# One PSUM tile of eight banks for a whole transformer-block kernel, in place of three pools

## The chip, the cores and the metric

The kernel runs on one core of one Trainium2 chip. The metric is device time in microseconds of one execution. Five engines matter: PE (TensorE) multiplies matrices and writes its sums to PSUM; DVE (VectorE), ACT (ScalarE) and POOL (GpSimd) compute on elements; SP (SyncE) issues most of the DMA transfers. PSUM has eight banks of 512 float32 per partition; one matmul of this kernel fills at most one bank.

## The reference, cut to what matters

One layer with 512 latent tokens, 256 context tokens and model width 2048, in float32. The work is a chain of large matrix products with two mixers between:

```python
cos, sin = _axial_rope_tables(n_lat)
h = _modulate(_rmsnorm(x, norm_g), shift, scale)        # of latent and context tokens
p = h @ w_in                  # q, k, v, z_a (gate of A), u_b, z_b (gate of B), g_a, g_b
q, k = _rope(_rmsnorm(q)), _rope(_rmsnorm(k))           # per head; 12 query, 4 key heads
attn = softmax(q @ k.T) @ v
y_a = (attn * silu(z_a)) @ w_pa
y_b = (_fourier_mix(u_b) * silu(z_b)) @ w_pb
y = (sigmoid(g_a) * y_a + sigmoid(g_b) * y_b) @ w_o     # then gated residual, final norm
```

## The kernel before

**Products.** Each float32 operand is split into a high and a low half (ACT writes the high one, `whi` or `s`, at L181; DVE the low one, `wlo` or `s`, at L182), and one float32 product becomes three matmuls: high x high (L338), high x low (L339), low x high (L340) in `mm3`. The input projection is done by Winograd's form of a 2x2 block product, seven half-size products with sums and differences around them, for one group of 512 columns at a time. Group g takes its products in the order P1, Q5, P2, Q6, P7, Q3, Q4 (class `Group`). P1 and P2 add up in one accumulator, "a"; Q5, Q6 and Q3 in "b"; P7 and Q4 in "c". Every accumulator is a pair of banks, one bank for each 128 rows. A product is 48 matmuls of 512 columns into one pair.

**The groups.** Groups 0 to 2 hold a quarter of the query heads and of the gate z_a ("qz"), groups 3, 4, 6 and 7 hold g_a and g_b ("gate"), group 5 keys and values ("kv"). When Q4 of a qz group is done, DVE takes its sum from PSUM (L1128, `ev<-x,ev`, the reader of accumulator "c"), and `rotated` (norm and rotation, L1233 to L1241) follows. One half of Q3's and P7's results passes through a tanh, for which `qz_done` takes a scratch pair of banks (`e = pair(...)`, ACT L1249, DVE L1250).

**What hands out banks.** There are three stages, each with a PSUM pool of its own. Stage 1 (modulation, the start of the projection, the Fourier mix) uses the pool `ps` with single banks in three kinds: b1 four times (`bank`), b2 twice (`bank2`), b3 twice (`bank3`). The groups use the pool `psp`: a tag `x` of two pairs, from which the framework gives out whichever is due, and the tags `y0` and `y1`. From the attention on, the pool `psq` is one tile of all eight banks, `banks`; `pair` slices it by turns and the framework follows the readers and writers of each part. Accumulators "a" and "c" are x pairs, "b" a y pair. Before a pool opens, the earlier one is closed, and work on it has to be finished for what comes to lie there.

**What sets the order of the work.** A scheduler of the framework takes the instructions as the program emits them, and orders each engine's list ahead of time by its estimate of when each may start; so a wait that it foresees lets it put other instructions ahead. On the chip each engine goes through its list in order. PE, DVE and ACT wait for one another's counts; DMA issues stand in the lists too. Weights come as raw tiles (`wr`, `R`; issued at L217, L220 on SP and L291 on POOL), are partly added up on DVE (L269), are split and are then used by PE. `wr<-in_ctx_toks` (the context tokens, four pieces) are read during group 2 for their norm on ACT (L1331).

Of the kernel before, what the change touches and what calls it, by code (L numbers as in the profile page):

```python
# [10 lines left out]
F32 = mybir.dt.float32  # L11
# [4 lines left out]
PSUM = bass.MemoryType.PSUM  # L16
DRAM = bass.MemoryType.DRAM

P = 128
# [104 lines left out]
def block_kernel(ctx, tc, xT, ctx_rows, ctx_toks, x, c_row, w_ss, w_gate, vecs, qkg, rope, dft_c, dft_s,  # L124
# [4 lines left out]
    def region(name, side="left", **kw):  # L129
        st = ExitStack()  # L130
        return st, st.enter_context(tc.tile_pool(name=name, bufs=1, side=side, **kw))
# [18 lines left out]
    b_d = dsc.tile([2, P, 2, T], F32, name="b_d")  # L150
    g_d = dsc.tile([2, 2, 4, P, 1024], F32, name="g_d")
    yb_d = dsc.tile([2, 4, P, 1024], F32, name="yb_d")
    pss, ps = region("ps", None, space=PSUM)

    cnt = [0]

    def uid(s):
        cnt[0] += 1
        return f"{s}{cnt[0]}"
# [8 lines left out]
    def hm_tile(shape, dt, name):  # L168
        return slot(hm, shape[1:], dt)

    def bank(shape=(P, 512)):
        return ps.tile(list(shape), F32, tag="b1", bufs=4, name=uid("pb"))

    def bank2():
        return ps.tile([P, 512], F32, tag="b2", bufs=2, name=uid("pd"))

    def bank3():
        return ps.tile([P, 512], F32, tag="b3", bufs=2, name=uid("pc"))

    def split_from(src, hi, lo):  # L180
        first = nc.scalar.activation(hi, src, ACT.Copy)  # L181
# [239 lines left out]
    for g in range(LAST + 1):  # L421
        for name in ONE_GROUP:
            if (g, name) == (LAST, "Q4"):
                stream_keys(0)
            if g == KV:
                f = CTX_FORMS.index(next(f for n, f, _, _ in PRODUCTS if n == name))
# [94 lines left out]
    fsq = [ppool.tile([P, 2, 2, FREQ], F32R, name="fsq0")]  # L521
    rx = pap.tile([P, T], F32, name="rx")
    wacc = bank3()
    def warm(n, src):

# [3 lines left out]
    def token_norms():  # L529

        t = hm_tile([P, 2, T], F32, name=uid("nm"))
        pick, r = t[:, 0, :].rearrange("p (t c) -> p t c", t=4), t[:, 1, :P]
        nc.gpsimd.memset(pick, 0.0)
        for t in range(4):
            nc.gpsimd.memset(pick[32 * t : 32 * t + 1, t, :], 1.0)
        acc = bank2()
        for q in range(0, KK, 2):
            two = hm_tile([P, 2, T], F32, name=uid("sq"))
            a, b = two[:, 0, :], two[:, 1, :]
            nc.scalar.activation(a, xt[:, q, :], ACT.Square)  # L540
            if q in (6, 10):
                nc.vector.tensor_tensor(b, xt[:, q + 1, :], xt[:, q + 1, :], op=ALU.mult)
            else:
                nc.scalar.activation(b, xt[:, q + 1, :], ACT.Square)
            nc.vector.tensor_tensor(a, a, b, op=ALU.add)
            for t in range(4):
                nc.tensor.matmul(acc[32 * t : 32 * t + 32, :P], ones[:, :32], a[:, t * P : t * P + P],
                                 start=q == 0, stop=q == KK - 2)
            if q < KK - 4:
                warm(1, two[:, 0, :256])  # L550

        nc.scalar.activation(r, acc[:, :P], ACT.Sqrt, bias=eps_t[:, 0:1], scale=1.0 / D)
        nc.vector.reciprocal(r, r)
        return pick, r

    def spread(pick, r):
        acc = bank3()
        for t in range(4):
            nc.tensor.matmul(acc[:, t * P : t * P + P], pick[:, t, :], r, start=True, stop=True)
        return acc  # L560
# [12 lines left out]
    def modulate(kb, meanwhile=lambda: None):  # L573
        two[kb] = bank2()
        for h in range(2):
            matvec(kb, h)
        meanwhile()
        return taken(kb)

    def modulate_pair(kb, loads):  # L580
        two[kb] = two[kb + 1] = bank2()
        for i in range(2):
            for h in range(2):
                matvec(kb + i, h, i == 0, i == 1)
            if i:
                taken(kb)
            wada.pop(kb + i, None)
            loads(kb + i)
# [91 lines left out]

    def start_work():
        sums_u = [bank() for _ in range(4)]
        for p in start_pieces():
            kb, nk, t, nt = p[2:]
# [111 lines left out]
    with tc.manual_schedule(engines={E.PE}):  # L796
# [6 lines left out]
        with tc.manual_schedule(engines={E.Activation, E.DVE}):  # L803
# [25 lines left out]
            for kb in range(1, 4):  # L829
                k = kb + 1  # L830
# [32 lines left out]
            for kb in range(4, KK - 4, 2):  # L863
# [6 lines left out]
                k = kb + 2  # L870
# [79 lines left out]
    def positions(g):  # L950

        ah, al = AH.pop(g)
        acc = [bank()[:, :FREQ] for _ in range(2)]
        for i, v in ((0, ah), (1, ah), (0, al)):
            for r, o in enumerate(acc):
                nc.tensor.matmul(o, fch[:, i, P * r : P * r + P], v[:, r, :], start=i == 0 and v is ah, stop=v is al,
                                 skip_group_check=True)
        z = part[:, 4 + g, :]
        y, odd = (fnp.tile([P, n], F32, tag=t, bufs=4, name=uid(t)) for t, n in (("y", T), ("odd", FREQ)))
        nc.scalar.copy(odd, acc[1])  # L960
        nc.vector.tensor_tensor(y[:, :257], acc[0][:, :257], odd[:, :257], op=ALU.subtract)
        nc.vector.tensor_tensor(y[:, 257:], acc[0][:, 255:0:-1], odd[:, 255:0:-1], op=ALU.add)
        products.append((z, y))
# [22 lines left out]
    pst.close()  # L986


    pss.close()
    fm2 = ctx.enter_context(tc.tile_pool(name="fm2", bufs=1, reuse_waits="tile"))  # L990
    fms = [fm] * 4 + [fm2] * (KK - 4)
    turn_fm = [4]
    evs, evp = region("evp", "right", reuse_waits="tile")
    new_ev = lambda: evp.tile([P, 2, 512], F32, tag="ev", bufs=4, name=uid("ev"))
    qzs, qzp = region("qzp", "right", reuse_waits="tile")
    pgs, psp = region("psp", None, space=PSUM, reuse_waits="tile")
    last_y = [0]

    banks = []
    rows4 = lambda hi, lo: [(hi[:, j, :], lo[:, j, :]) for j in range(4)]  # L1000

    def make_form(f, h):
# [22 lines left out]
    def pair(tag, skip=0):  # L1025
        if isinstance(tag, int):
            return banks[0][:, tag : tag + 2, :] if tag < 6 else banks[1]
        if banks:
            last_y[tag == "x"] += 1
            b = 2 * (last_y[tag == "x"] % 2) + (4 if tag == "y" else 0)  # L1030
            return banks[0][:, b : b + 2, :] if b < 6 else banks[1]
        if tag == "y":
            last_y[0] += 1 + skip
            return psp.tile([P, 2, 512], F32, tag=f"y{last_y[0] % 2}", bufs=1, name=uid(tag))
        return psp.tile([P, 2, 512], F32, tag=tag, bufs=2, name=uid(tag))


    forms = {"A11": [(hhi[j][:, :256], hlo[j][:, :256]) for j in range(8)],
# [17 lines left out]
    class Banks:  # L1056


        def __init__(self):
            self.b = [pair("x") for _ in range(2)]  # L1060
# [4 lines left out]
    class Group:  # L1065
# [16 lines left out]
        def steps(self, name):  # L1082
# [5 lines left out]
            if start:  # L1088

                self.acc[which] = Banks() if (self.last or self.g == LAST) and which == "c" else pair(self.tags[which])  # L1090
# [385 lines left out]
    ats_, atp = region("atp", "right", reuse_waits="tile")  # L1476


    pgs.close()
    psq = ctx.enter_context(tc.tile_pool(name="psq", bufs=1, space=PSUM, reuse_waits="tile"))  # L1480
    whole_psum = psq.tile([P, 8, 512], F32, name="banks")
    banks += [whole_psum[:, :6, :], whole_psum[:, 6:, :]]
    last_y[:] = [0, 0]
    wide = [flat(banks[0])[:, NKEY * i : NKEY * i + NKEY] for i in range(4)]
    fill_acc, b1 = banks[1][:, 0, :], lambda: banks[1][:, 1, :]
# [219 lines left out]
    for i in range(NSTEP + 3):  # L1705
# [21 lines left out]
        n = next((n for n, at in enumerate(SUM_AT) if at <= i < at + 3), None)  # L1727
# [19 lines left out]
        if i in GATE_STEPS:  # L1747
            n = NGATE + GATE_STEPS.index(i)
# [6 lines left out]
        if i == NSTEP - 1:  # L1755
            a_groups.append(a_group(0))
            first = a_groups[0].steps("P1")
# [333 lines left out]
```

## Time and profile before

| | us |
|---|---|
| median of 3 runs | 1285.03 (1284.46 to 1285.83) |
| the profiled execution | 1286.17 |
| its span, first to last instruction | 1284.4 |
| PE busy in the span | 1269.6 (99%) |
| DVE busy | 989.9 (77%) |
| ACT busy | 680.9 (53%) |
| mean granted TensorE clock | 0.996 |

The profiled execution stands 1.14 us above the median, and 1.8 us of it lie outside its span. Stage 1 lasts until 153 us; groups 0 to 7 from 153 to 804; the attention follows, then the two branch projections and the output product. In a row of the timeline, 229.54 0.39 PE is an instruction that started at 229.54 us and took 0.39 us; matmuls overlap, and in the groups one starts 0.2267 us after the other (48 matmuls from 305.70 to 316.58).

### The profile page before, as it was taken

The numbers are of one execution on the slowest core, as the hardware profiler recorded it, in microseconds if no ns is written. First come the engines' busy times: TensorE is split into PE (matmuls) and PEld (weight loads), VectorE is DVE, ScalarE is ACT, GpSimd is POOL, SyncE is SP. The second block draws the span as 40 slices with busy tenths as digits, with TensorE's granted clock in tenths as the row PEclk, the third lists the DMA queues.
The fourth block names the chain that finished last, engine by engine and source line by source line (L and its number), as shares of the span: only waits on it lengthen the run. The fifth ranks groups of instructions, "written<-read, shape, count | busy, mean of one in ns | idle before, by whom it ended". The sixth has DMA issues, their size and how long they took to land.

```text
span 1284.4 us, 17614 instructions
## 1 busy us (share of the span) xinstructions
PE 1269.6 (99%) x6554; PEld 1045.1 (81%) x6554; DVE 989.9 (77%) x1302; ACT 680.9 (53%) x1073; POOL 175.9 (14%) x229
## 2 busy tenths in 40 slices
PE   8999999999999999999999999999999999999997
PEld 5677888888888888888888888888888888788886
DVE  5767899889778787748687656788798777787677
ACT  5322765555456464443354545666677646465544
POOL 0000121111102011012031010021100221211310
PEclk8999999999999999999999999999999999999999
DMA  9998798888898998877879797588762989998986
GB/s 377 405 374 346 244 205 254 229 240 234 236 306 222 299 288 258 290 199 181 285 200 309 234 253 234 174 240 264 250 191 82 249 240 257 247 200 232 218 209 181
DMA packets 104422, 319.07 MB, mean 248 GB/s; under 512 B 9968, under 2 KB 32880, under 8 KB 100368
## 3 DMA queue, kind: packets, MB, share of 16 engines
q1 hardware_dynamic: 54336, 195.24, 42.1%
q0 software_dynamic: 27680, 100.29, 36.8%
q10 hardware_dynamic: 22320, 22.42, 5.1%
q8 instruction: 51, 0.84, 0.2%
q14 instruction: 35, 0.29, 0.1%
HBM read 283.30 MB, written 34.61 MB: 248 GB/s over the span
## 4 chain that ended last, share of the span: by engine, by line
PE 96%; DMA 1%; DVE 1%; ACT 1%; issue 1%; POOL 0%; SPq 0%; DVEq 0%; ACTq 0%
PE banks L338 11%; PE banks L340 10%; PE banks L339 10%; PE x L339 9%; PE x L340 9%; PE x L338 9%; PE y L339 8%; PE y L340 8%; PE y L338 8%; PE banks L1570 3%; PE pd L566 2%; PE pc L338 1%; PE pb L338 1%; PE pc L340 1%; PE pc L339 1%; PE pb L339 1%
## 5 line engine op out<-in xcount | busy, mean ns | idle before, releaser
L181 ACT ACTIVATE whi<-R 128x1024 fp32r<-128x1024 f32 x138 | 145.3, 1058 | 141.7 <-PE banks L340 49.3
L182 DVE TENSOR_TENSOR wlo<-R,whi 128x1024 fp32r<-128x1024 f32 x138 | 168.0, 1223 | 58.9 <-ACT whi L181 58.9
L182 DVE TENSOR_TENSOR wlo<-wr,whi 128x1024 fp32r<-128x1024 f32 (+1 forms) x122 | 147.5, 1215 | 64.5 <-ACT whi L181 64.4
L181 ACT ACTIVATE whi<-wr 128x1024 fp32r<-128x1024 f32 (+1 forms) x122 | 127.2, 1050 | 119.9 <-PE y L340 36.2
L338 PE MATMUL banks<-whi,s 128*128 128x512 f32 (+1 forms) x400 | 157.1, 393 | 0.7 <-ACT ev L1179 0.7
L340 PE MATMUL banks<-whi,s 128*128 128x512 f32 (+1 forms) x400 | 156.3, 391 | 0.0
L339 PE MATMUL banks<-wlo,s 128*128 128x512 f32 (+1 forms) x400 | 156.1, 390 | 0.0
L339 PE MATMUL x<-wlo,s 128*128 128x512 f32 x352 | 137.1, 389 | 0.2 <-DVE wlo L182 0.2
L338 PE MATMUL x<-whi,s 128*128 128x512 f32 x352 | 137.1, 390 | 0.0
L340 PE MATMUL x<-whi,s 128*128 128x512 f32 x352 | 137.0, 389 | 0.0
L291 POOL DMA_DIRECT2D R<-in_w_g x68 | 59.3, 873 | 481.5 <-DVE wlo L182 219.9
L339 PE MATMUL y<-wlo,s 128*128 128x512 f32 x316 | 123.2, 390 | 0.0
L338 PE MATMUL y<-whi,s 128*128 128x512 f32 x316 | 123.0, 389 | 0.0
L340 PE MATMUL y<-whi,s 128*128 128x512 f32 x316 | 122.8, 389 | 0.0
L181 ACT ACTIVATE s<-wr 128x512 fp32r<-128x512 f32 (+2 forms) x93 | 60.4, 676 | 67.0 <-DMA wr<-cf_d 23.9
L182 DVE TENSOR_TENSOR s<-wr,s 128x512 fp32r<-128x512 f32 (+2 forms) x93 | 66.9, 752 | 31.4 <-ACT s L181 30.4
L338 PEld LDWEIGHTS banks<-whi,s 128*128 128x128 f32 x400 | 75.2, 188 | 16.5 <-ACT ev L1179 1.1
L340 PEld LDWEIGHTS banks<-whi,s 128*128 128x128 f32 x400 | 75.2, 188 | 14.9
L339 PEld LDWEIGHTS banks<-wlo,s 128*128 128x128 f32 x400 | 75.2, 188 | 14.0 <-DVE wlo L182 0.2
L339 PEld LDWEIGHTS x<-wlo,s 128*128 128x128 f32 x352 | 66.1, 188 | 14.3 <-DVE wlo L182 0.8
L338 PEld LDWEIGHTS x<-whi,s 128*128 128x128 f32 x352 | 66.1, 188 | 13.7
L340 PEld LDWEIGHTS x<-whi,s 128*128 128x128 f32 x352 | 66.1, 188 | 13.7
(334 smaller groups left out, 2796.2 us busy)
## 6 DMA issues: line engine op xcount, KB each, us to landing
wr<-in_w_g SPq DMA_DIRECT2D x124, 512.0 KB, 5.6
R<-in_w_g POOLq DMA_DIRECT2D x68, 512.0 KB, 7.4
wa<-in_w_ss SPq DMA_DIRECT2D x31, 1024.0 KB, 9.1
R<-in_w_g SPq DMA_DIRECT2D x32, 512.0 KB, 5.6
wr<-in_w_gate SPq DMA_DIRECT2D x32, 512.0 KB, 4.9
wr<-in_w_o SPq DMA_DIRECT2D x24, 512.0 KB, 6.9
R<-in_w_o POOLq DMA_DIRECT2D x24, 512.0 KB, 8.6
wr<-in_w_pab SPq DMA_DIRECT2D x20, 512.0 KB, 5.3
```

Of the source, the lines that this page charges most:

```text
L181: first = nc.scalar.activation(hi, src, ACT.Copy)
L182: return first, nc.vector.tensor_tensor(lo, src, hi.bitcast(F32), op=ALU.subtract)
L291: chained[:] = [nc.gpsimd.dma_start(chain[e.pc], e.nxt, accum_op=ALU.add)]
L338: nc.tensor.matmul(o, ah, bh, start=start, stop=False, skip_group_check=cont)
L339: nc.tensor.matmul(o, ah, bl, start=False, stop=False, skip_group_check=cont)
L340: nc.tensor.matmul(o, al, bh, start=False, stop=stop, skip_group_check=cont)
L566: nc.tensor.matmul(acc[32 * j : 32 * j + 32], c[:, n, :], w[:, k, :], start=first and n < 4, stop=last and n >= KK - 4, skip_group_check=n ...
L1570: nc.tensor.transpose(tp[:, k * P : (k + 1) * P], p[:, k * P : (k + 1) * P], ident)
```

## The change

All eight banks are one tile, `banks`, from the start. Stage 1's three functions take their single banks from it by turns: banks 0 to 3, 4 and 5, 6 and 7. The groups' `pair("x")` takes banks 2:4 and 0:2 alternately, `pair("y")` 6:8 and 4:6 alternately. The attention and what follows use the same tile with the same slices as before. Closing and opening of pools is gone.

```diff
@@ block_kernel
-    pss, ps = region("ps", None, space=PSUM)
+    whole_psum = ctx.enter_context(tc.tile_pool(name="ps", bufs=1, space=PSUM)).tile([P, 8, 512], F32, name="banks")
+    in_turn = {}
@@
-    def bank(shape=(P, 512)):
-        return ps.tile(list(shape), F32, tag="b1", bufs=4, name=uid("pb"))
+    def turned_bank(first, n):
+        k = in_turn[first] = (in_turn.get(first, -1) + 1) % n
+        return whole_psum[:, first + k, :]
+
+    def bank():
+        return turned_bank(0, 4)
 
     def bank2():
-        return ps.tile([P, 512], F32, tag="b2", bufs=2, name=uid("pd"))
+        return turned_bank(4, 2)
 
     def bank3():
-        return ps.tile([P, 512], F32, tag="b3", bufs=2, name=uid("pc"))
+        return turned_bank(6, 2)
@@
-    pss.close()
...
-    pgs, psp = region("psp", None, space=PSUM, reuse_waits="tile")
-    last_y = [0]
-
-    banks = []
+    last_y = [0, 0]
+
+    banks = [whole_psum[:, :6, :], whole_psum[:, 6:, :]]
@@ def pair(tag, skip=0)
-        if banks:
-            last_y[tag == "x"] += 1
-            b = 2 * (last_y[tag == "x"] % 2) + (4 if tag == "y" else 0)
-            return banks[0][:, b : b + 2, :] if b < 6 else banks[1]
-        if tag == "y":
-            last_y[0] += 1 + skip
-            return psp.tile([P, 2, 512], F32, tag=f"y{last_y[0] % 2}", bufs=1, name=uid(tag))
-        return psp.tile([P, 2, 512], F32, tag=tag, bufs=2, name=uid(tag))
+        last_y[tag == "x"] += 1 + skip
+        b = 2 * (last_y[tag == "x"] % 2) + (4 if tag == "y" else 0)
+        return banks[0][:, b : b + 2, :] if b < 6 else banks[1]
@@ where the attention begins
-    pgs.close()
-    psq = ctx.enter_context(tc.tile_pool(name="psq", bufs=1, space=PSUM, reuse_waits="tile"))
-    whole_psum = psq.tile([P, 8, 512], F32, name="banks")
-    banks += [whole_psum[:, :6, :], whole_psum[:, 6:, :]]
```

Each engine has the same instructions as before (PE 6245, DVE 1271, ACT 993, POOL 234, SP 358); their banks, waits and places in the lists differ. 51 of PE's, 77 of DVE's, 70 of ACT's, 11 of POOL's and 3 of SP's stand at another place. All line numbers in the text are those of the kernel before; in the changed one L338 to L340 are L343 to L345, L1128 is L1126, L181 and L182 are L186 and L187, and L269 is L274.

The first place is on PE, where group 0 ends and group 1 begins. `x_1938` is the pair in which Q4 of group 0 adds up (its last matmuls), `x_2191` the pair of group 1's P1; `whi`, `wlo` are halves of weights, the numbered `s` halves of the tokens. Before:

```order
L339 MATMUL x_1938<-wlo_2099,s_1213 128x512
L340 MATMUL x_1938<-whi_2098,s_1214 128x512
L338 MATMUL x_2191<-whi_2117,s_286 128x512 [waits Activation_49]
L339 MATMUL x_2191<-wlo_2118,s_286 128x512 [waits DVE_49]
L340 MATMUL x_2191<-whi_2117,s_287 128x512
```

Now (`whi_2131` is a weight of group 1's Q5, `whi_2037` of its P1):

```order
L344 MATMUL banks<-wlo_2019,s_1164 128x512
L345 MATMUL banks<-whi_2018,s_1165 128x512
L343 MATMUL banks<-whi_2131,s_1550 128x512 [waits Activation_49]
L343 MATMUL banks<-whi_2131,s_1550 128x512
L343 MATMUL banks<-whi_2037,s_283 128x512 [waits DVE_49]
L344 MATMUL banks<-wlo_2038,s_283 128x512
```

Two matmuls of Q5, which were 48 places further on, stand ahead of P1, and P1's first matmul waits for a DVE instruction: it is L1128 (now L1126), the subtraction that reads Q4's sum, since P1's pair is the one that Q4 wrote. Where group 1 ends and group 2 begins the same wait stands behind eight matmuls of Q5, and where group 2 ends and group 3 begins behind two.

The second place is on DVE at the end of group 2. `ev_2914<-x_3094` is that subtraction, `R` a sum of weight pieces. Before:

```order
L269 TENSOR_TENSOR R_1312<-R_1312,wr_3357 128x1024 [waits DMAHW7_49,DVE_49]
L182 TENSOR_TENSOR wlo_3342<-R_1313,whi_3341 128x1024 [waits DMAHW3_49,Activation_49]
L269 TENSOR_TENSOR R_1313<-R_1313,wr_3397 128x1024 [waits DMAHW7_49,DVE_49]
L182 TENSOR_TENSOR wlo_3363<-R_1314,whi_3362 128x1024 [waits DMAHW4_49,Activation_49]
L269 TENSOR_TENSOR R_1314<-R_1314,wr_3441 128x1024 [waits DMAHW5_49,DVE_49]
L1128 TENSOR_TENSOR ev_2914<-x_3094,ev_2914 128x1024 [waits PE_49]
L182 TENSOR_TENSOR wlo_3380<-R_1311,whi_3379 128x1024 [waits Activation_49]
```

Now:

```order
L274 TENSOR_TENSOR R_1262<-R_1262,wr_3261 128x1024 [waits DVE_49]
L187 TENSOR_TENSOR wlo_3246<-R_1263,whi_3245 128x1024 [waits DMAHW3_49,Activation_49]
L274 TENSOR_TENSOR R_1263<-R_1263,wr_3301 128x1024 [waits DMAHW1_49,DVE_49]
L187 TENSOR_TENSOR wlo_3267<-R_1264,whi_3266 128x1024 [waits DMAHW4_49,Activation_49]
L1126 TENSOR_TENSOR ev_2824<-banks,ev_2824 128x1024 [waits PE_49]
L187 TENSOR_TENSOR wlo_3284<-R_1261,whi_3283 128x1024 [waits Activation_49]
```

One addition (`R_1314`, now `R_1264`) has moved behind the subtraction; all else ahead of it is the same. At the ends of groups 0 and 1 the subtraction has the same instructions of DVE ahead of it as before.

## The prediction

> **What bounds the kernel now.** First the page's busy times and clock, then the chain of waits, then the waits of PE, last PE's load stage by stage.
>
> ```profile
> span 1284.4 us, 17614 instructions
> PE 1269.6 (99%) x6554; PEld 1045.1 (81%) x6554; DVE 989.9 (77%) x1302; ACT 680.9 (53%) x1073; POOL 175.9 (14%) x229
> PEclk8999999999999999999999999999999999999999
> PE 96%; DMA 1%; DVE 1%; ACT 1%; issue 1%; POOL 0%; SPq 0%; DVEq 0%; ACTq 0%
> ```
>
> PE is busy for 99% of the span, and 96% of the chain that ends last is PE. Any pause of PE counts in full, unless PE waits later for something that is not late too. How much it waits now stands in the waits of PE (total, times, longest) and, by stage, in the windows (after the length of the stretch, busy us of PE, PEld, DVE, ACT and POOL; granted clock; DMA share; GB/s).
>
> ```profile
> PE banks L1684 <- DMA s<-yb_d: 1.1, 1, 1.1
> PE banks L338 <- ACT ev L1179: 0.7, 1, 0.7
> PE x L339 <- DVE wlo L182: 0.2, 1, 0.2
> 150.00:800.00 650.00, 649.81 (x2883) 537.27 (x2882) 505.44 (x619) 332.19 (x531) 90.81 (x102) 1.00 0.87 247
> 800.00:1000.00 200.00, 199.24 (x1310) 174.68 (x1309) 168.40 (x271) 137.23 (x263) 26.08 (x43) 1.00 0.65 201
> ```
>
> From 150 to 800 us, the groups, PE lacks 0.19 of 650 us. There is nothing to gain there, only to lose, and an added wait cannot hide behind one that is there. DVE, with 505 of 650, has room, but works in order.
>
> **The instructions themselves: nothing.** The same instructions run, on tiles of the same shape, so busy times stay. What costs or gains is who waits for whom at five places. In stage 1, until 153 us, the single banks go by the same number of turns as before; I take zero.
>
> **Place 1, the first group (153 us).** P1 of group 0 now gets banks 2 and 3, which the Fourier mix's last step still reads.
>
> ```profile
> 153.03 0.40 PE L338 MATMUL x<-whi,s 128*128 128x512 f32 x1
> 153.23 0.38 ACT L960 COPY odd<-pb 128x258 f32<-128x258 f32 x1 [0.41 <-PE pb L956]
> 155.87 0.42 DVE L962 TENSOR_TENSOR y<-pb,odd 128x255 f32<-128x255 f32 x1
> ```
>
> The list now has 13 matmuls into bank 3 first, which wait for the copy (ends 153.61), then those into bank 2, which wait for L962 (ends 156.29). From an end to its waiter's start takes about 0.05 (L1179 and L338 below). The first starts at 153.66 instead of 153.03: **+0.6**. One matmul starts about 0.2267 after the other (229.32 and 229.54 below are such a step), so thirteen end that stretch at 156.6, after 156.29, so the second wait costs nothing.
>
> Behind it the scheduler permutes DVE's list between 166 and 205 us. One low split is pulled ahead of the pair L1012 and waits for its ACT half:
>
> ```profile
> 166.49 1.29 DVE L1012 TENSOR_TENSOR S<-s,S 128x512 f32<-128x512 f32 x2
> 168.31 1.23 DVE L182 TENSOR_TENSOR wlo<-R,whi 128x1024 fp32r<-128x1024 f32 x1 [0.53 <-ACT whi L181]
> 206.77 1.24 DVE L182 TENSOR_TENSOR s<-S,s 128x1024 fp32r<-128x1024 f32 x1
> 208.06 0.50 PE L340 MATMUL y<-s,s 128*128 128x512 f32 x1
> ```
>
> If the pair's 1.29 then runs after the split, DVE is that much late, until the split at 206.77, for which the matmul at 208.06 waits with 0.05 to spare. PE being 0.6 late already, 0.6 to 0.7 remain: **+0.7**, between 0 (a gap in DVE's list swallows it) and 1.3. PE is then 1.3 late.
>
> **Place 2, the end of group 0.** P1 of group 1 gets the pair whose Q4 sum DVE has yet to subtract.
>
> ```profile
> 229.32 0.39 PE L340 MATMUL x<-whi,s 128*128 128x512 f32 x1
> 229.54 0.39 PE L338 MATMUL x<-whi,s 128*128 128x512 f32 x1
> 229.67 1.22 DVE L182 TENSOR_TENSOR wlo<-R,whi 128x1024 fp32r<-128x1024 f32 x1
> 230.92 1.23 DVE L269 TENSOR_TENSOR R<-R,wr 128x1024 f32<-128x1024 f32 x1
> 232.07 1.22 DVE L1128 TENSOR_TENSOR ev<-x,ev 128x1024 f32<-128x1024 f32 x1
> ```
>
> Q4's last matmul is that of 229.32, P1's first that of 229.54. The subtraction starts 2.3 us later, since a split and an addition stand ahead of it, and ends at 233.29; P1 could start at 233.34. Two Q5 matmuls (0.45) fill some of the pause. PE's lateness after it is 233.34 - 229.54 - 0.45 = 3.35, if DVE is on its old schedule, and 3.35 + 1.3 = 4.65 if DVE is as late as PE. DVE came late out of place 1 but has other work to wait on; I take half, 0.65: **PE is 4.0 late**. Behind P1 on PE stands the whole of group 1, and everything that waits for it.
>
> **Place 3, the end of group 1.**
>
> ```profile
> 305.70 0.39 PE L338 MATMUL x<-whi,s 128*128 128x512 f32 x1
> 306.25 1.22 DVE L1128 TENSOR_TENSOR ev<-x,ev 128x1024 f32<-128x1024 f32 x1
> ```
>
> Here the subtraction follows 0.55 us after the old P1, and eight Q5 matmuls (1.81) are put ahead: 305.70 + 1.81 = 307.51 against 307.47 + 0.05. **Zero** if DVE moves with PE, and also if PE alone is late; 0.2 at most.
>
> **Place 4, the end of group 2.**
>
> ```profile
> 378.13 1.06 ACT L1331 ACTIVATE wr<-wr 128x1024 f32<-128x1024 f32 x1 [5.14 <-DMA wr<-in_ctx_toks]
> 380.23 1.23 DVE L1250 SCALAR_TENSOR_TENSOR ev<-y,ev 128x1024 f32<-128x1024 f32 x1 [3.24 <-ACT y L1249]
> 381.86 0.39 PE L338 MATMUL x<-s 128*128 128x512 f32 x1
> 387.48 1.23 DVE L269 TENSOR_TENSOR R<-R,wr 128x1024 f32<-128x1024 f32 x1
> 388.62 1.22 DVE L1128 TENSOR_TENSOR ev<-x,ev 128x1024 f32<-128x1024 f32 x1
> ```
>
> This is the dear one: the subtraction starts 6.8 us after P1's old start, since DVE is behind. ACT had to wait 5.14 us for the context tokens, and DVE 3.24 for ACT. The addition of 387.48 has moved behind the subtraction, which thus starts at 387.48, ends at 388.70, and P1 starts at 388.75; less two matmuls put ahead, PE is 388.75 - 381.86 - 0.45 = **6.4 late, plus what DVE itself is late by then**. That lies between 0 (the transfer sets DVE's time, and is on its old schedule) and the full 4.0. What the transfer waits for:
>
> ```profile
> 354.44 0.39 PE L340 MATMUL x<-whi,s 128*128 128x512 f32 x1
> 356.55 1.06 ACT L181 ACTIVATE whi<-wr 128x1024 fp32r<-128x1024 f32 x1 [1.78 <-DVE ev L1128]
> 358.73 0.33 SPq L217 DMA_DIRECT2D wr<-in_ctx_toks  x1
> 349.00 0.39 PE L340 MATMUL y<-whi,s 128*128 128x512 f32 x1
> 352.76 1.06 ACT L181 ACTIVATE whi<-wr 128x1024 fp32r<-128x1024 f32 x1 [2.55 <-DMA wr<-in_w_g]
> ```
>
> SP issues the first piece when a raw tile is split; the split's buffer comes free with the matmul of 354.44, which ended 1.7 us before ACT began. The split before had 3.4 us to spare and was waiting for a transfer. A PE that is 4.0 late makes the first 2.3 late and the second 0.6. I take the mean, **1.5**: PE is 7.9 late after group 2.
>
> After that the gate groups take only two x pairs each, so that turns and readers do not meet, and the kv group's three do not end on a pair in use.
>
> **Place 5, the attention.**
>
> ```profile
> 803.59 0.58 ACT L1179 COPY ev<-x 128x512 f32<-128x512 f32 x1 [1.66 <-PE x L340]
> 804.23 0.50 PE L338 MATMUL banks<-whi,s 128*128 128x512 f32 x1 [0.68 <-ACT ev L1179]
> ```
>
> PE waited 0.68 for the last copy out of a pool that had to close. Now the first matmuls go to a bank that was free, and those into the bank copied come nine later: **-0.7**. The one wait of 0.2 for a low split (657 us) gains a high matmul ahead of it: **-0.2**.
>
> **Sum.** 7.9 - 0.9 = +7.0 on the profiled execution's 1286.17. The profiled execution stands 1.14 above the median, and the difference belongs to the median as well: 1285.03 + 7.0 = **1292.0**. With no lateness of DVE at places 2 and 4 it is 6.4 - 0.9 = 5.5, or 1290.5; with full lateness 4.65 after place 2, 11.1 after place 4, +10.2, or 1295.2.
>
> **Two rules of the Trainium skill.** The pauses of PE are some 2.7 us at place 2 and about 4 at place 4 (7.9 - 4.0). The one long pause of the trace lies at its start (a row of PE, then windows as above):
>
> ```profile
> 7.17 0.43 PE L547 MATMUL pd<-s,ones 128*32 128x128 f32 x8 [2.35 <-DVE s L545]
> 8.30:15.10 6.80, 6.65 (x40) 2.82 (x40) 4.76 (x8) 5.23 (x10) 0.00 (x0) 0.50 1.04 416
> 15.10:22.00 6.90, 5.80 (x72) 3.48 (x72) 2.99 (x6) 1.69 (x5) 0.00 (x0) 1.00 1.02 405
> ```
>
> After 2.35 us without work, the granted clock was 0.50 for 6.8 us. If a pause at places 2 or 4 does the same, PE does half its work for 6.8 us and loses 3.4; at place 2, most of that is taken back at place 4, where the subtraction sets the start, so one loss counts: **+1.7** for half that stretch, **+3.4** for all. The Trainium skill has that on "TensorE: Matmul & The Clock Gate" (Why this matters for your kernels): no idle gap of PE over about 3 us, or the clock goes to half. By that rule place 2 would pass and place 4 would not. The trace has the half clock behind a shorter pause, of 2.35 us, with little work ahead of it.
>
> The Trainium skill's "Perfetto Trace Analysis" (Optimizing Tensor Performance, Matmuls) says that independent groups of matmuls should rotate through different banks, so that the reading of one runs beside the next. The rows of places 2 and 4 agree: the old P1 started 2.5 and 6.8 us ahead of the read. By the rule alone the change is a loss, of the size that those rows give.
>
> **The rivals.**
>
> *All moves with PE* (0.17): DVE is as late as PE at each place, 1295.2. For it: DVE's list is in order and fed by splits that PE's progress frees. Against: the 5.14 for a transfer.
>
> *The clock halves after a pause* (0.18): 1293.7 to 1295.4. For it: the start of the trace; against: that pause followed little work, not a full PE.
>
> *The transfer catches up* (0.12): while PE stands still, fewer transfers compete, the context tokens land earlier, and DVE's idle 3.24 at 380.23 goes. Place 4 then takes only 6.4 - 3.2 = 3.2, less than the lateness of 4.0 from place 2, and adds nothing: 4.0 - 0.9 = +3.1, or 1288.1.
>
> *Not slower: the lateness is given back* (0.06). If the attention (800 to 1000 us) runs on transfers and exponentials that do not wait for the groups, a late PE finds all ready and 7.9 is taken back: 1285.03 - 0.9 = 1284.1. It decides only if PE's 199.24 busy of 200 us hide waits of 7.9, as ends of matmuls are modelled; ACT is busier there than elsewhere. Against: scores start from PE's own sums.
>
> *The change does not do what it says* (0.02, the old time): the three subtractions are named in the lists of waits, so I leave little.
>
> **How the numbers follow.** The forecast (1290.5 to 1293.5) has 0.45. The range reaches from the catch-up to full lateness with half a halved clock (11.1 - 0.9 + 1.7 = 11.9): 1288.0 to 1296.9, with the last two rivals left out. Within 0.2% (2.6 us, about what a measurement of this kernel can tell from no change) needs most of the lateness gone: 0.08 from the last two rivals and 0.02 from a catch-up that goes further, 0.10 in all. Faster: 0.02, since no case gives 2.6. Slower: the rest, 0.88.
>
> **What would show it.** Right: a wait of PE for L1128 at two places of the after profile, about 2.7 us before group 1 and 4 before group 3, none or a trace before group 2; place 5's 0.68 gone; no other new wait. The row of L1128 at group 2's end stands right ahead of P1. Wrong: a half clock behind a pause, a wait of under 1 us at either place, or PE's total wait going up by less than 4.

## The result and the profile after

| | before | changed |
|---|---|---|
| median, us | 1285.03 | 1304.59 (1304.35 to 1307.88) |
| ratio | 1 | 1.0159 (95% interval 1.0145 to 1.0173) |
| span of the profiled execution, us | 1284.4 | 1304.0 |

The changed kernel is 19.6 us slower. The forecast was 7.0 us slower (1292.0), the range ended at 1296.9: right in the direction, and too small by a factor of nearly three.

The page of the changed kernel, in the same parts as before:

```profile
span 1304.0 us, 17590 instructions
PE 1276.2 (98%) x6554; PEld 1047.2 (80%) x6554; DVE 990.6 (76%) x1302; ACT 680.2 (52%) x1073; POOL 170.9 (13%) x229
PEclk9999999999998999999999999999999999999999
PE 48%; DMA 3%; DVE 2%; ACT 1%; issue 1%; POOL 1%; ACTq 0%; DVEq 0%; SPq 0%; POOLq 0%
```

DVE and ACT are as busy as before to within 1 us, so no work was added. PE is busy for 6.6 us more, with the same matmuls: some ran slower, and the clock's digit 8 in the 13th slice (391 to 424 us) shows one of the places. The chain of the last line could be followed back to 603 us only (its shares add up to 56%), so it is not read here. PE's waits (total, times, longest):

```profile
PE banks L343 <- ACT whi L186: 7.4, 3, 6.0
PE banks L343 <- DVE ev L1126: 3.4, 2, 1.9
PE banks L344 <- DVE wlo L187: 2.5, 2, 1.8
...
PE banks L343 <- ACT odd L965: 0.5, 1, 0.5
...
PE banks L1678 <- DMA s<-yb_d: 0.3, 1, 0.3
```

The old 0.7 for the pool that closed is gone, 1.1 for `yb_d` has become 0.3, and three kinds of wait have come: for the subtraction L1126, for high halves of weights, and for low halves. Where they stand is seen from the starts of matmuls that have the same place in PE's list in both traces:

| matmul at, before | at, changed | PE late by | what lies between |
|---|---|---|---|
| 205.08 | 206.95 | 1.9 | place 1 and the list behind it |
| 241.33 | 247.85 | 6.5 | place 2, end of group 0 |
| 318.85 | 325.74 | 6.9 | place 3, end of group 1 |
| 393.65 | 411.41 | 17.8 | place 4, end of group 2 |
| 616.75 | 635.96 | 19.2 | a low half comes late |
| 661.43 | 682.35 | 20.9 | a low half comes late |
| 804.23 | 824.04 | 19.8 | start of the attention |
| 1119.96 | 1139.31 | 19.4 | the wait for `yb_d` |

Place 2 in the timeline of the changed kernel (start, duration, instruction, wait before it):

```profile
231.12 0.39 PE L345 MATMUL banks<-whi,s 128*128 128x512 f32 x1
232.71 0.73 PE L343 MATMUL banks<-whi,s 128*128 128x512 f32 x2 [1.20 <-ACT whi L186]
234.95 0.80 PE L343 MATMUL banks<-whi,s 128*128 128x512 f32 x1 [1.50 <-DVE ev L1126]
235.54 0.63 PE L344 MATMUL banks<-wlo,s 128*128 128x512 f32 x1
238.08 0.40 PE L344 MATMUL banks<-wlo,s 128*128 128x512 f32 x1
233.67 1.22 DVE L1126 TENSOR_TENSOR ev<-banks,ev 128x1024 f32<-128x1024 f32 x1
233.00:237.00 4.00, 2.50 (x7) 1.67 (x7) 4.00 (x5) 2.07 (x15) 0.68 (x1) 0.70 0.82 258
237.00:244.00 7.00, 7.00 (x31) 5.69 (x29) 6.27 (x10) 3.19 (x7) 3.33 (x4) 0.93 0.61 101
```

The two Q5 matmuls that were put ahead, then P1 right behind L1126, which is 1.6 us later than before (233.67 against 232.07), nearly as late as PE is there (1.8: Q4's last matmul is at 231.12 instead of 229.32). After the pause matmuls take 0.63 and start 0.43 apart until 238.1, then 0.39 again; the last two rows are windows, with the granted clock 0.70 and 0.93. P1's first matmul is 5.4 late (234.95 against 229.54), of which the two Q5 matmuls, already done, give back 0.45: 4.95. Behind the slow matmuls PE is 6.5 late, so they cost some 1.6.

Place 4:

```profile
388.70 0.39 PE L345 MATMUL banks<-whi,s 128*128 128x512 f32 x1
395.10 1.22 PE L343 MATMUL banks<-whi,s 128*128 128x512 f32 x2 [6.01 <-ACT whi L186]
398.21 0.79 PE L343 MATMUL banks<-s 128*128 128x512 f32 x1 [1.89 <-DVE ev L1126]
398.80 0.63 PE L344 MATMUL banks<-s,s 128*128 128x512 f32 x1
402.07 0.39 PE L343 MATMUL banks<-s,s 128*128 128x512 f32 x1
387.71 1.06 ACT L1329 ACTIVATE wr<-wr 128x1024 f32<-128x1024 f32 x1 [5.81 <-DMA wr<-in_ctx_toks]
396.94 1.22 DVE L1126 TENSOR_TENSOR ev<-banks,ev 128x1024 f32<-128x1024 f32 x1
395.30:398.40 3.10, 1.21 (x3) 0.49 (x4) 3.10 (x4) 0.21 (x1) 0.00 (x0) 0.50 0.78 250
```

PE stands from 389 to 398, with two Q5 matmuls at 395 that had to wait for their own weights' high half. The subtraction is still what ends last, right ahead of P1, but it starts at 396.94: 9.5 us later than the 387.48 that the forecast started from, while PE came there 7.1 late (Q4's last matmul at 388.70 instead of 381.64). The step that I let be an estimate, how late DVE is, is the one that was wrong.

### The profile page after: what moved, and what is told of

Read it like the earlier page. It is cut to its first block, busy times and chain, and to the rows that moved or that the text cites. A ratio compares the mean times of both kernels' runs of the same rounds, so it can differ in the third digit from the quotient of the medians.

```text
span 1304.0 us, 17590 instructions
## 1 busy us (share of the span) xinstructions
PE 1276.2 (98%) x6554; PEld 1047.2 (80%) x6554; DVE 990.6 (76%) x1302; ACT 680.2 (52%) x1073; POOL 170.9 (13%) x229
## 4 chain that ended last, share of the span: by engine, by line
PE 48%; DMA 3%; DVE 2%; ACT 1%; issue 1%; POOL 1%; ACTq 0%; DVEq 0%; SPq 0%; POOLq 0%
PE banks L343 15%; PE banks L344 15%; PE banks L345 14%; PE banks L1564 3%; DMA s<-yb_d 1%; DMA wr<-in_w_g 1%; DVE wlo L187 1%; DMA R<-in_w_pab 1%; PE banks L1678 0%; POOL small L1220 0%; PE banks L1413 0%; PE banks L1579 0%; ACT whi L186 0%; PE banks L1406 0%; ACT banks L1231 0%
## 5 line engine op out<-in xcount | busy, mean ns | idle before, releaser
L343 PE MATMUL banks<-whi,s 128*128 128x512 f32 (+1 forms) x1129 | 442.4, 393 | 9.4 <-ACT whi L186 7.4
L344 PE MATMUL banks<-wlo,s 128*128 128x512 f32 (+1 forms) x1129 | 440.7, 390 | 2.5 <-DVE wlo L187 2.5
L345 PE MATMUL banks<-whi,s 128*128 128x512 f32 (+1 forms) x1129 | 439.9, 390 | 0.0
L343 PEld LDWEIGHTS banks<-whi,s 128*128 128x128 f32 x1129 | 212.4, 188 | 56.8 <-ACT whi L186 8.7
L344 PEld LDWEIGHTS banks<-wlo,s 128*128 128x128 f32 x1129 | 212.5, 188 | 45.8 <-DVE wlo L187 4.3
L345 PEld LDWEIGHTS banks<-whi,s 128*128 128x128 f32 x1129 | 212.3, 188 | 43.4
L186 ACT ACTIVATE whi<-R 128x1024 fp32r<-128x1024 f32 x138 | 145.0, 1058 | 148.2 <-PE banks L345 120.3
L187 DVE TENSOR_TENSOR wlo<-R,whi 128x1024 fp32r<-128x1024 f32 x138 | 167.6, 1221 | 60.9 <-ACT whi L186 60.7
L187 DVE TENSOR_TENSOR wlo<-wr,whi 128x1024 fp32r<-128x1024 f32 (+1 forms) x122 | 147.0, 1212 | 71.7 <-ACT whi L186 71.5
L186 ACT ACTIVATE whi<-wr 128x1024 fp32r<-128x1024 f32 (+1 forms) x122 | 127.4, 1051 | 140.1 <-PE banks L345 71.7
L344 PE MATMUL banks<-s,s 128*128 128x512 f32 (+1 forms) x444 | 168.8, 380 | 0.7 <-DVE s L187 0.6
L345 PE MATMUL banks<-s,s 128*128 128x512 f32 (+1 forms) x444 | 168.3, 379 | 0.0
L343 PE MATMUL banks<-s,s 128*128 128x512 f32 (+1 forms) x434 | 166.5, 385 | 0.0
L186 ACT ACTIVATE s<-wr 128x512 fp32r<-128x512 f32 (+2 forms) x93 | 60.9, 677 | 74.2 <-DMA wr<-in_w_g 23.4
L344 PEld LDWEIGHTS banks<-s,s 128*128 128x128 f32 x444 | 83.9, 189 | 16.3 <-DVE s L187 1.4
L187 DVE TENSOR_TENSOR s<-wr,s 128x512 fp32r<-128x512 f32 (+2 forms) x93 | 67.4, 749 | 38.5 <-ACT s L186 38.2
L343 PEld LDWEIGHTS banks<-s,s 128*128 128x128 f32 x434 | 81.7, 188 | 18.5 <-ACT s L1548 2.0
L345 PEld LDWEIGHTS banks<-s,s 128*128 128x128 f32 x444 | 83.9, 189 | 15.0
L186 ACT ACTIVATE s<-R 128x512 fp32r<-128x512 f32 (+1 forms) x84 | 54.5, 668 | 36.3 <-PE banks L345 25.9
L187 DVE TENSOR_TENSOR s<-R,s 128x512 fp32r<-128x512 f32 (+1 forms) x84 | 60.1, 736 | 14.0 <-ACT s L186 13.6
L282 DVE TENSOR_TENSOR wr<-R,wr 128x1024 f32<-128x1024 f32 x40 | 48.6, 1219 | 20.3 <-DMA wr<-in_w_g 16.8
```

The costliest lines, as they stand in the source:

```text
L187: return first, nc.vector.tensor_tensor(lo, src, hi.bitcast(F32), op=ALU.subtract)
L282: nc.vector.tensor_tensor(src, chain[e.pc], src, op=ALU.subtract)
L343: nc.tensor.matmul(o, ah, bh, start=start, stop=False, skip_group_check=cont)
L344: nc.tensor.matmul(o, ah, bl, start=False, stop=False, skip_group_check=cont)
L345: nc.tensor.matmul(o, al, bh, start=False, stop=stop, skip_group_check=cont)
```

## The experiments

All times are medians; each ratio is against the kernel before, run beside it (1284.5 to 1285.0), with its 95% interval. Theory A says that P1's two waits are the loss. Theory B says that the lists of DVE and ACT, in another order, cost by themselves.

### No pair handed out while it is read

```diff
-... else pair(self.tags[which])
+... else pair(self.tags[which], int(name == "P1" and self.g in (1, 2, 3)))
```

> The changed kernel, but P1 of groups 1, 2 and 3 takes the x pair after the next, so that it gets the pair that the pool of the kernel before gave it and no longer the pair that Q4 has just filled. Theory A (P1's waits for the subtraction at the ends of groups 0 and 2, 4.9 and 10.9 us of PE's lateness in the changed kernel's trace, are the loss): both waits go; what stays is 1.9 from the first group, 3.1 at 617 and 658 us and a gain of 2.2 at the attention and at 1120: 1285.0 + 2.8 = 1287.8, no wait of PE for L1126. Theory B (the lists of DVE and ACT, in which the rotation's steps now stand ahead of weight splits, cost by themselves): DVE is several us late at 350 us without any wait on PE, and a pause of PE of 3 us or more stays before group 3: 1291 or more.

Measured: 1291.02, ratio 1.0053 (1.0038 to 1.0067). The waits for L1126 are gone, and of the 19.6 us 6.1 are left. PE's waits in this kernel:

```profile
PE banks L344 <- DVE wlo L187: 4.3, 5, 1.8
```

At 351.06 and 354.81 us, without any pause of PE before, it waits 0.4 and 0.7 for low halves, then at three more places. So both theories have a part: the time is theory B's, but the pause of 3 us before group 3 that it asked for is not there. The DVE list of the kernel before at that stretch, with one row of ACT, and then this one's:

```profile
343.47 1.22 DVE L182 TENSOR_TENSOR wlo<-wr,whi 128x1024 fp32r<-128x1024 f32 x1
344.60 0.69 DVE L1235 TENSOR_TENSOR qr<-x,qr 128x512 f32<-128x512 f32 x1
345.20 0.43 DVE L1237 TENSOR_TENSOR y<-x,qr 128x256 f32<-128x256 f32 x1
...
347.01 1.22 DVE L182 TENSOR_TENSOR wlo<-wr,whi 128x1024 fp32r<-128x1024 f32 x1
348.14 1.29 DVE L182 TENSOR_TENSOR s<-wr,s 128x512 fp32r<-128x512 f32 x2
349.35 0.69 DVE L1235 TENSOR_TENSOR qr<-x,qr 128x512 f32<-128x512 f32 x1
347.20 0.26 ACT L1233 ACTIVATE y<-x 128x128 f32<-128x128 f32 x1 [3.94 <-DVE y L1237]
```

```profile
346.33 1.22 DVE L187 TENSOR_TENSOR wlo<-R,whi 128x1024 fp32r<-128x1024 f32 x1
347.46 0.69 DVE L1233 TENSOR_TENSOR qr<-banks,qr 128x512 f32<-128x512 f32 x1
348.06 0.89 DVE L1235 TENSOR_TENSOR banks<-banks,qr 128x256 f32<-128x256 f32 x2
348.87 0.68 DVE L1233 TENSOR_TENSOR qr<-banks,qr 128x512 f32<-128x512 f32 x1
349.46 0.42 DVE L1235 TENSOR_TENSOR banks<-banks,qr 128x256 f32<-128x256 f32 x1
349.80 1.22 DVE L187 TENSOR_TENSOR wlo<-wr,whi 128x1024 fp32r<-128x1024 f32 x1
```

L1235 and L1237 (now L1233 and L1235) are the products of `rotated`, three for its first half and then three for its second. Before, the split `wlo<-wr` at 343.47 stands ahead of both halves, and three more splits ahead of the second. Now both halves but for their last product stand ahead of it. The reason is in the waits: before, ACT's squares for the second half (they write the other bank of the same pair) waited for DVE's products of the first, at 347.20 after 3.94 us (the first fence's last row); with parts of one tile they don't (in this kernel all eight squares follow one another from 338.76 on, with one split between), so the second half is ready sooner. That the scheduler puts it in sooner for this reason is put to the test below, by a dependency that brings the wait back.

### And group 0 in a free pair too

```diff
-    last_y = [0, 0]
+    last_y = [0, 1]
```

> As the run before, and the x turns also start one pair further on, so that P1 of group 0 gets banks 0 and 1 in place of 2 and 3, which the Fourier mix's last step reads. Theory A: the 1.9 us of the first group go too: 1286 (1285 to 1287), PE starts group 0 at 153.0. Theory B: the wait of 0.6 at 153 goes, the rest of the first run's loss stays.

Measured: 1293.32, ratio 1.0074 (1.0054 to 1.0094). The wait of 0.5 at 153 us is gone, but the time is no better than the first run's. Waits for low halves total 4.7 us there, the longest 3.3, behind which the clock was at half for 6.8 us (more on that in the last section): the order of the lists decides, not the wait at place 1.

### One part of the change alone

```diff
 (the kernel before, and from group 0 on)
+    whole_psum = psq.tile([P, 8, 512], F32, name="banks")   # with the changed pair()
 (the kernel before, and in stage 1)
+    stage1 = ps.tile([P, 8, 512], F32, name="banks")        # with turned_bank()
```

> The kernel before with only its second and third pool joined: one tile of eight banks from group 0 on with the turns of the changed kernel, stage 1 with its own pool. Theory A: the waits at the ends of groups 0 and 2 are all there, only the first group's 1.9 us are not: 1304.6 - 1.9 = 1302.7. If the first group's lateness is what puts DVE behind at the later places, less: below 1298.

> The kernel before with only stage 1 changed: its eight single banks are parts of one tile by turns, the two later pools as before. Both theories: no change, 1285.0 within 1 us, since PE's waits of stage 1 are the same in both traces to within 0.3 us.

Measured: 1305.05, ratio 1.0159 (1.0144 to 1.0174) for the groups, and 1290.02, ratio 1.0042 (1.0026 to 1.0059) for stage 1. Both expectations missed, by the same wait, first in the groups' kernel, then in stage 1's:

```profile
PE banks L338 <- DVE y L962: 3.2, 1, 3.2
```

```profile
PE x L344 <- DVE y L968: 3.2, 1, 3.2
156.16 0.47 PE L344 MATMUL x<-whi,s 128*128 128x512 f32 x1 [3.22 <-DVE y L968]
```

Either way the first matmul of group 0 waits until the last reader of stage 1 is done (L968 is the old L962). So in these two kernels, where the tile on one side of a closing pool spans all eight banks, the first user of the new pool waits for the last reader of the old one. The changed kernel has the one tile on both sides, and waits only 0.5 there. Stage 1 alone has the same order of instructions as the kernel before on PE, DVE, ACT and POOL, and this wait is the only new one of PE in its trace; but the trace shows only 1.4 of lateness left behind the wait for `yb_d`, it is that of the fastest execution (1287.48), and the median is 5.1 slower. The greater part of that loss stays unexplained.

### The old interleaving, by one dependency

```diff
+    held = const.tile([P, 1], F32, name="held")
     def rotated(half, v, t2):
...
                 nc.scalar.activation(t2[:, b, h, :], v[:, b, h, :], ACT.Square,
+                                     **({"bias": held} if b and not h else {}),
...
+            if not b:
+                with tc.issue_after(turned.ins):          # turned: the last product of the first half
+                    nc.vector.memset(held, 0.0)
```

> The first run (no pair handed out while it is read) with one dependency added: in the rotation, ACT's squares of the second half read a zero that DVE writes after its products of the first half (six memsets of one column). In the kernel before, a wait for those products stood there by itself; in the changed one it does not, and the eight products of the rotation stand together on DVE, ahead of a weight split. With the dependency DVE's list has the old interleaving again. Order theory (the first run's 6.1 us are weight splits that stand behind the rotation): 1285 to 1287, waits of PE for low splits back under 1 us from 4.3. If the order is not it: 1291, as the first run.

> The changed kernel with that dependency alone; P1 of groups 1 to 3 still gets the pair that Q4 has just filled. If the two causes add up: 1304.6 - 6.1 = 1298.5. If the order is also what made the end of group 2 dear (a wait there of 6.0 us for a weight split and 1.9 for the subtraction), that pause falls to about 4 us and the time to 1293 to 1297. If the pauses do not depend on the order: above 1300.

> The dependency, no pair handed out while it is read, and P1 of group 0 in banks 0 and 1 too. Order theory: as the first kernel of this call or up to 1 us less, 1284 to 1286.5; the second run of the first call (1293.3) lost 4.7 us to low splits, and these go. Otherwise 1293.

| | turns as changed | no pair while it is read |
|---|---|---|
| order as changed | 1304.59 (1.0159) | 1291.02 (1.0053) |
| old interleaving | 1302.55 (1.0140; 1.0124 to 1.0155) | 1285.11 (1.0004; 0.9995 to 1.0014) |

Above the kernel before that ran beside each, that is 19.6 and 6.1 us in the first row, 18.0 and 0.6 in the second. With both causes away nothing is left of the loss that can be measured: one tile throughout is as fast as three pools, and the order theory's 1285 to 1287 came. With group 0 in a free pair besides it is 1285.21 (1.0005; 0.9996 to 1.0015), so the wait at place 1 costs nothing that can be measured. In the kernel of 1285.11, PE's waits for low halves of weights (`wlo`) are off the list of PE's waits, from 4.3. The order alone costs 5.5 us more than that (6.1 - 0.6), the two pairs alone 17.4, and both 19.0, less than the sum. A PE that waits at places 2 and 4 no longer waits for three of the five low halves of the first run (0.44, 0.71 and 0.77 us, at 351, 355 and 406 us there), and behind place 4 it is 17.8 late with the changed order and 17.7 with the old one; so the two rows 616.75 and 661.43 of the table at the top are what the order still costs there. None of these beats the kernel before.

Place 4 with the old interleaving and the turns as changed, in the kernel of 1302.55:

```profile
393.58 1.22 PE L343 MATMUL banks<-whi,s 128*128 128x512 f32 x2 [4.45 <-ACT whi L186]
397.96 0.79 PE L343 MATMUL banks<-s 128*128 128x512 f32 x1 [3.16 <-DVE ev L1126]
366.74 1.46 SPq L222 DMA_DIRECT2D wr<-in_ctx_toks  x2
385.90 1.06 ACT L1335 ACTIVATE wr<-wr 128x1024 f32<-128x1024 f32 x1 [4.93 <-DMA wr<-in_ctx_toks]
396.69 1.22 DVE L1126 TENSOR_TENSOR ev<-banks,ev 128x1024 f32<-128x1024 f32 x1
```

PE was 7.1 late on arrival. The first piece of the context tokens was issued at 366.74 instead of 358.73, 8.0 late; ACT's use of the last at 385.90 instead of 378.13, 7.8 late; the subtraction at 396.69 instead of 388.62, 8.1 late. DVE is late in full, and so is the transfer. The expectation of 1293 to 1297, that the dear pause comes from the order, fell, and so did the sum 1298.5; what came is the third, above 1300.

The same lateness in four kernels with the old interleaving, in which PE comes to place 4 early or late (the first and the last are those of the next section):

| kernel | Q4's last matmul (before: 381.64) | ACT's use of the last piece (378.13) | subtraction (388.62) |
|---|---|---|---|
| place 4 alone, 1297.91 | 0.7 late | 0.6 late | 0.9 late |
| no pair while it is read, 1285.11 | 2.1 | 2.8 | 3.1 |
| both places, 1302.55 | 7.1 | 7.8 | 8.1 |
| place 2 alone, 1290.70 | 7.6 | 8.7 | 9.0 |

So in these DVE is as late as PE at this place, and 0.2 to 1.3 us more, whether PE then waits for it or not. ACT's wait for the last piece is 4.08, 5.50, 4.93 and 4.66 us in these, 5.14 before: it does not shrink as PE gets later.

### The two places apart

```diff
 (the changed kernel; first alone, and the other two with the dependency)
+ pair(self.tags[which], int(name == "P1" and self.g == 3))     # place 4 away; with and without the dependency
+ pair(self.tags[which], int(name == "P1" and self.g == 1))     # place 2 away
```

> The changed kernel, but P1 of group 3 alone takes the x pair after the next, so that only the wait at the end of group 2 is taken away; the order of the rotation stays. If that pause (10.9 us of lateness in the changed kernel's trace, half clock included) stands by itself: 1304.6 - 10.9 = 1293.7. If its greater part is lateness of the weight splits, which stays and shows as other waits: 1296 to 1300.

> The changed kernel with the old interleaving of the rotation (the added dependency), and P1 of group 1 in the free pair: of the two dear waits only that at the end of group 2 is left. PE then comes to it 1.9 us late or less. If DVE at that place is as late as PE in full (the subtraction at 388.62 + 1.9, P1 at 391.8): PE is 9.5 late behind it, a half clock adds about 1.8, the attention gives 2 back: 1294. If DVE's late stand there had only been the transfer's: 1.5 less. If what was lost at the end of group 0 had been taken back at this place, as the prediction has it: the time is that of the kernel with both waits, 1302.

> The changed kernel with the old interleaving, and P1 of group 3 in the free pair: only the wait at the end of group 0 is left. It leaves PE 6.9 us late in the trace with both (half clock included). If lateness is never given back but where PE waited before (2 us at the attention): 1284.7 + 6.9 - 2 = 1289.6, and this excess and that of the run before add up to that of both, 17.4. If the groups take it back: 1286 or less.

Measured, in that order: 1298.02 (ratio 1.0096; 1.0078 to 1.0114), 1297.91 (1.0096; 1.0080 to 1.0111) and 1290.70 (1.0045; 1.0030 to 1.0060). With the order as changed, taking place 4 away leaves 13.5 of the 19.6 us, so it saves 6.1 and not 10.9, as the second expectation had it: low halves then cost 6.3 of waiting, the longest 3.3. With the old interleaving the two places alone cost 13.0 and 5.8, together 18.7, against 18.0 with both (1302.55 against 1284.52). So the price of place 2 stays to the end, and is not taken back at place 4. In the traces PE comes out of place 4 alone 11.1 late, having come 0.7 late, and out of place 2 alone 7.2 late, having come 1.4 late. The expectation for place 2 alone (1289.6) missed by 1.1. That for place 4 alone (1294) fits the profiled execution, 1294.48, but the other three took 1297.2 to 1298.7; what they lost besides has no trace, so this price is good to some 2 us at best.

### The pauses filled

```diff
+            if start and name == "P1" and self.g in (1, 3):
+                spare = pair((2 * ((last_y[0] + 1) % 2)) + 4)
+                ah = self.forms[form][0][0]
+                for _ in range(20 if self.g == 1 else 48):
+                    nc.tensor.matmul(spare[:, 0, :256], ah[:, :P], ah, start=True, stop=True, ...)
```

> The changed kernel with the old interleaving and both waits, and matmuls that serve nothing put into the pauses: 20 of 256 columns ahead of P1 of group 1, 48 ahead of P1 of group 3, into the y pair that Q5 overwrites; the result is not touched. Clock theory (the half clock behind each pause, rows of 0.63 in place of 0.39, comes from PE's standing still and costs some 1.8 us each time): the granted clock stays at 1.00 at both places, and the time falls from 1302.5 to about 1299. If the half clock comes from something else, or P1's start is not moved by it: 1302 or more.

Measured: 1300.45, ratio 1.0114 (1.0097 to 1.0131). That is 15.5 us above the kernel before, against 18.0 without them (1.0140; 1.0124 to 1.0155); the two intervals overlap. Its timeline and windows at the two places:

```profile
232.99 2.55 PE L1094 MATMUL banks<-s 128*128 128x256 f32 x20
237.15 0.47 PE L343 MATMUL banks<-whi,s 128*128 128x512 f32 x1 [1.60 <-DVE ev L1131]
229.00:245.00 16.00, 14.40 (x74) 12.17 (x73) 14.56 (x20) 8.89 (x24) 2.94 (x4) 1.00 0.73 196
390.97 6.02 PE L1094 MATMUL banks<-s 128*128 128x256 f32 x48 [0.87 <-DVE ev L1259]
399.44 0.77 PE L343 MATMUL banks<-s 128*128 128x512 f32 x1 [2.46 <-DVE ev L1131]
400.00 0.63 PE L344 MATMUL banks<-s,s 128*128 128x512 f32 x1
380.00:405.00 25.00, 21.68 (x112) 18.36 (x111) 19.18 (x24) 12.84 (x30) 3.15 (x5) 0.93 0.86 278
```

At place 2 the pause shrinks to 1.60, and the clock stays at 1.00; PE loses 4.3 us there instead of 5.6. At place 4 a pause of 2.46 is left, and the rows of 0.63 are back. So the theory is borne out at the first place, in one trace, and was not put to the test at the second; a gain of some 2 of the expected 3.5 would fit one of two, but is not clear of the noise. That a pause must halve the clock does not follow, as the last section shows.

## Why the prediction was wrong, point by point

**What bounds the kernel** held: PE's pauses count in full, but for what comes back where PE waited before. Of 20.9 us of lateness at 661 us 1.1 came back by the start of the attention and 0.5 more by the wait for `yb_d`; in the four traces of the table above with the old interleaving 2.8 to 3.0 came back from 617 us on.

**Place 1**, +1.3: the wait of 0.6 at 153 us came (0.5 in the list of waits), and PE was 1.9 late at 207. The wait has no price in the end: without it PE is as late at the end of group 0 (2.0 against 2.1 us), from waits for splits at 170 and 206 us, and the time is the same (1285.21 against 1285.11).

**Place 2**, +2.7: measured 4.7 (1.86 to 6.52 late). Two terms failed. DVE's lateness, taken as half (0.65), was nearly full: the subtraction was 1.6 late, PE 1.8, and 3.35 + 1.60 is the 4.95 of P1's first matmul. And the half clock, which I left to a rival with a chance of 0.18, came; P1's matmuls from 234.95 to 238.1 lost 1.6 us by it, and those at place 4 lost 1.9 (15.9 late at P1's start, the two Q5 matmuls deducted, 17.8 behind it). That a loss here is taken back at place 4, as the prediction argued for the half clock, is wrong too: PE came to place 4 7.1 late, and DVE with it.

**Place 3**, zero, 0.2 at most: measured 0.4 (6.52 to 6.89). Right in the main: eight matmuls filled the time until the subtraction, and no wait for L1126 is listed there.

**Place 4**, +3.9: measured 10.9. This is the step that failed most. "What DVE itself is late by then" was taken as 1.5, the mean of what the slack of two splits would leave of PE's 4.0; it was 9.5. The form of the sum was right: 6.4 + 9.5 = 15.9 is how late P1 started, and the half clock's 1.9 makes it 17.8, where the forecast had 6.4 + 1.5 = 7.9. So this one term is 8.0 of the 12.6 us by which the forecast fell short. The 5.14 us in which ACT waits for the context tokens had looked like a schedule of the transfer's own. It is not: SP issues the pieces when raw tiles come free (of SP's waits in the kernel before, 410.6 us in 94 are for low splits), the splits write into buffers that PE has to release, and with PE 7.1 late the issue was 8.0 late, and the wait for the transfer stayed at 4.93. The slack of 1.7 and 3.4 that I read in two rows did not hold anything back: in the four traces above the subtraction was never less late than PE. The rival that had everything move with PE was right in this, and I gave it 0.17. In the changed kernel the rotation ahead of the splits adds to it, 9.5 in place of 8.1, and the addition that moved behind the subtraction takes 1.1 off, as written; so the subtraction starts at 396.94 there and at 396.69 with the old interleaving.

**The order of the lists.** Besides the addition at place 4, the prediction prices permutations of DVE's list between 166 and 205 us only. The list also moved around the rotations, at the ends of groups 0 to 2 and in the kv group, and the price of that was taken as zero without a row. Alone it is 5.5 us; in the changed kernel, at 617 and 661 us, +3.2 (17.76 to 20.92 late), where the forecast had -0.2. At 661 us L1239 of the rotation now stands at 677.09, ahead of the split at 678.23 for which PE waits 1.76, where before the split came first.

**Place 5**, -0.7: measured -1.1 from 661 us to the attention (20.9 to 19.8), with the 0.68 gone from the waits. Right.

**The signs.** The waits for L1126 came at two places, of 1.50 and 1.89 us, each behind another wait of the two Q5 matmuls (1.20 and 6.01), and none ahead of group 2. Of the signs of being wrong, the half clock behind a pause came.

**Rotation and the half clock.** The Trainium skill's page "Perfetto Trace Analysis" (Optimizing Tensor Performance, Matmuls) has independent groups of matmuls rotate through different banks so that the reading of one overlaps the next; the runs agree, with the number that the pairs give: 17.4 us for two places at which they did not. The Trainium skill's page "TensorE: Matmul & The Clock Gate" (Why this matters for your kernels) names idle gaps of over about 3 us. Here pauses of 1.20 and 1.50 with two matmuls between, and one of 2.46 behind light work, were enough, and two of 3.22 and 3.31 went without.

**The rivals.** "All moves with PE" and "the clock halves" both happened. The range had them together with half of the halved clock (11.9); with all of it they make 11.1 - 0.9 + 3.4 = 13.6, or 1298.6, outside the range. What that still lacks is above all that DVE was 9.5 late at place 4 and not the 4.65 of that rival, and the order's 3.2 at 617 and 661 us. "The transfer catches up" and "given back" did not happen.

## What to carry to other kernels

In a kernel whose engines feed one another through a few buffers, a late PE makes the loads late as well: a wait for a transfer that stands in the trace is no reserve unless the transfer's issue waits for nothing that PE releases. Turns by a fixed rule over two parts of one tile go wrong where a group takes an odd number, here three x pairs ("a", "c" and the scratch pair): ask, at each end of a group, which part is still being read, or let the group skip a turn. A change of how buffers are cut also changes which waits exist, and so the order that a scheduler writes; each place where the lists differ needs a price, and where there are many, the lists should be put back before anything else is measured.

## What the runs showed of the chip

At place 2 of the changed kernel, behind pauses of PE of 1.20 and 1.50 us with two matmuls between, the clock was granted at half for about 3.4 us (granted 0.70 over 4 us and 0.93 over the next 7 us, which at half makes 2.4 and 1.0 us), and the matmuls in it started 0.43 us apart instead of 0.23. So the two pauses cost 1.6 us more than the time in which PE stood still. After a pause of 2.46 us behind light matmuls the clock was half again, after one of 1.60 us it was not.

The length of a pause does not settle it. The kernels of 1293.32 and 1298.02 each wait 3.31 us for the same low half, and only the first has a half clock behind it; the row of the wait and a window behind it, first for the one, then for the other:

```profile
665.78 0.80 PE L344 MATMUL banks<-wlo,s 128*128 128x512 f32 x1 [3.31 <-DVE wlo L187]
665.10:671.80 6.70, 6.02 (x14) 4.78 (x15) 4.63 (x5) 1.35 (x2) 1.83 (x2) 0.50 1.01 243
672.85 0.50 PE L344 MATMUL banks<-wlo,s 128*128 128x512 f32 x1 [3.31 <-DVE wlo L187]
672.80:680.00 7.20, 7.15 (x31) 5.93 (x32) 6.78 (x8) 4.54 (x6) 2.68 (x3) 1.00 1.01 258
```

It is the same with the 3.2 us at the start of group 0: behind it the clock is 0.50 from 157.0 to 160.3 us where only the groups have the one tile, and 1.00 from 156.1 to 160 us where only stage 1 has it. What decides between them is not shown. So an experiment that moves a pause may gain or lose a half clock that it was not about; in the traces of the changed kernel it was worth 1.6 us at place 2 and 1.9 at place 4.
